# Four of eight condition sums as one-column products of TensorE, ahead of a hybrid attention and expert block

## The chip, the core and the metric

The kernel runs on one core of a Trainium2 chip. The metric is the device time of one execution in microseconds. A core has TensorE (PE in the rows, its weight loads as PEld), VectorE (DVE), ScalarE (ACT), GpSimd (POOL) and SyncE (SP), which issues most transfers; 16 DMA engines move the data.

## The reference

One transformer block for 512 tokens of 1,024 numbers. A condition c is turned into six rows; the first two shift and scale the first norm:

```
cs = silu(c)
mod = cs @ mod_w + mod_b
sh1, sc1, g1, sh2, sc2, g2 = split(mod, 6)
h = rms_norm(x, norm1_g) * (1 + sc1) + sh1
x = x + g1 * hybrid_mixer(h, w_in, ...)       # three kinds of attention, gates, output projection
h = rms_norm(x, norm2_g) * (1 + sc2) + sh2
x = x + g2 * moe_ffn(h, ...)                  # 32 experts, 4 for each token
return rms_norm(x, final_g)
```

mod_w is 1,024 x 6,144 in fp32. The case is about the first 2,048 of its columns: 1,024 sums for sh1 and 1,024 for sc1, each over 1,024 rows.

## The kernel before

**The condition.** `Mixer.start` (L743) loads the first 2,048 columns of mod_w in eight chunks of 1 MB: for each quarter k2 of the 1,024 columns first 256 scale columns, then 256 shift columns. So chunks 0, 2, 4 and 6 are scale, 1, 3, 5 and 7 are shift. The rows stand as eight pieces of 128 (k) on the partitions. Chunks 0, 1, 2, 4 and 6 lie in four small tiles each (z in the rows), 3 and 7 in p, 5 in o. For each chunk VectorE multiplies piece 0 by its column of cs (L786) and adds the other seven, each times its column, in seven scalar_tensor_tensor instructions (L784). This leaves a sum for each of 128 partitions; TensorE sums over the partitions by two fp32 products with a column of ones (L789), into columns of one tile `pc` in bank o. VectorE adds the bias (mc, L791) and, for scale columns, makes G1 = (1 + scale) * norm1_g (L793).

**What uses it.** x, normed by rows, is transposed by TensorE for each k (L798); ScalarE makes hT, the high part of (x * G1 + mc), for each k (L801), another instruction makes the full value (tp) and a subtraction the low part (L807). A quarter k2 gives two of the eight k.

**The projection.** Products of fp32 accuracy are made of three products of rounded fp32 parts (`mm3`, L632): high by high, low by high, high by low. `zT` (L944) makes one block of 128 columns: 8 k of 3 products, each 512 columns wide. The run (L1472) begins with four query blocks, two in banks z and two in banks s, then a key and a value block. Each needs its piece of w_in (raw), cast by ScalarE or VectorE to a high part and subtracted for a low one (`parts`, L814).

**Other work of VectorE.** `mod_steps` (L899) makes the other four rows of the condition in the same way, at a lower rank: eight steps of 1,024 columns for each row, from pieces called mraw, summed in acc.

**What sets the order.** All instructions up to the experts are first listed, then ordered by a planner (`Program.order`, L297). It simulates the engines with a list of prices (`price`, L263) and takes on each engine the earliest instruction that could start, by rank and then by place in the list; tiles get their place in the order in which they are first used (`access`, L243). The price of a product of plain fp32 is:

```
return max(0.107, n * 0.00168)
```

in us, for n columns. Every emitted instruction has line L417 in the profile. Banks: z has 2 places, s 3, t 2 (transposes), o 1. The bias columns of the projection are turned by TensorE in a bank s (L720).

After the mixer come the router and 32 experts, whose weights are streamed.

## Time and profile before

| | |
|---|---|
| median of 3 runs | 1854.42 us (1853.64 to 1858.9) |
| profiled execution | 1853.27 us, span 1851.3 us |
| PE busy | 1691.4 us (91%) |
| DVE busy | 1170.1 us (63%) |
| ACT busy | 764.9 us |
| POOL busy | 514.2 us |
| DMA | 512.38 MB, mean 277 GB/s |

Busy time is that of instructions on the engine; the ends of matmuls are modelled, and consecutive records overlap. [...]

### The profile page before, as it was taken

The page shows a single profiled execution, that of the slowest core. Times are in us where ns is not written, and L with a number is a line of the kernel's source. Part 1 is how long each engine was busy: PE and PEld are TensorE (multiplying, and loading weights), DVE is VectorE, ACT ScalarE, POOL GpSimd, SP SyncE. Part 2 cuts the span into 40 slices and gives each one's busy share as a digit, 9 for nine tenths or more (in the row PEclk, how much of TensorE's full clock was granted, in tenths as well). Part 3 has the DMA queues.
Part 4 walks back from the last instruction along what each step waited for, and adds up shares of the span by engine and source line. Part 5 has one row for each costly group of instructions (what it writes and reads, how often), then busy time and mean ns, then how long its engine had stood idle before and what let it go on. Part 6 is the DMA issues. An engine that isn't in the chain of part 4 may idle for free.

```text
span 1851.3 us, 22565 instructions
## 1 busy us (share of the span) xinstructions
PE 1691.4 (91%) x7923; PEld 1076.2 (58%) x7923; DVE 1170.1 (63%) x1797; ACT 764.9 (41%) x1081; POOL 514.2 (28%) x494
## 2 busy tenths in 40 slices
PE   4997999999999879897999998999899999989975
PEld 3776777777777766344445445455455455445654
DVE  7888768686865765346547546456475356435784
ACT  5473314474831234225426334335354235222652
POOL 5344202121212441311542221131131121412162
PEclk9999999999999979998999999999999999999997
DMA  9413465111133657999999999999999999999991
GB/s 323 153 61 114 117 198 164 58 46 58 47 95 103 238 191 283 402 398 377 374 397 399 340 363 352 385 376 395 404 387 354 363 372 394 373 402 407 408 358 47
DMA packets 156437, 512.38 MB, mean 277 GB/s; under 512 B 14266, under 2 KB 63545, under 8 KB 125601
## 3 DMA queue, kind: packets, MB, share of 16 engines
q1 hardware_dynamic: 146544, 486.65, 69.4%
q0 software_dynamic: 9136, 24.18, 5.4%
q8 instruction: 64, 1.05, 0.2%
q14 instruction: 53, 0.43, 0.1%
q10 hardware_dynamic: 640, 0.08, 0.0%
HBM read 492.81 MB, written 18.06 MB: 276 GB/s over the span
## 4 chain that ended last, share of the span: by engine, by line
PE 66%; DMA 14%; DVE 12%; ACT 4%; issue 2%; POOL 1%; SPq 0%; ACTq 0%; DVEq 0%; POOLq 0%
PE z L417 15%; PE hb L2041 7%; PE hb L1912 7%; PE hb L1914 6%; PE hb L1913 6%; DMA o<-in_exp_w_dram 6%; PE py L2041 5%; PE py L1914 3%; DMA raw<-in_exp_w_dram 3%; PE py L1912 3%; PE py L1913 3%; PE s L417 3%; DMA w<-in_exp_w_dram 2%; DVE z L417 2%; DVE p L417 2%
## 5 line engine op out<-in xcount | busy, mean ns | idle before, releaser
L417 PE MATMUL z<-hT,w 128*128 128x512 f32 (+1 forms) x1224 | 320.7, 403 | 3.3 <-DVE w L417 1.6
L417 PEld LDWEIGHTS z<-hT,w 128*128 128x128 f32 (+1 forms) x1224 | 225.2, 189 | 57.4 <-DVE w L417 3.5
L417 POOL TENSOR_TENSOR w<-raw,w 128x1024 fp32r<-128x1024 f32 (+2 forms) x32 | 63.6, 1990 | 160.6 <-ACT w L417 121.6
L1962 ACT CAST TH<-pt 128x512 fp32r<-128x512 f32 (+3 forms) x60 | 27.6, 510 | 189.4 <-PE pt L1961 189.4
L2041 PE MATMUL hb<-raw,T 128*64 128x512 f32 x448 | 102.8, 598 | 0.3 <-DMA raw<-in_exp_w_dram 0.3
L1912 PE MATMUL hb<-wh,TH 128*128 128x512 f32 (+3 forms) x256 | 103.1, 403 | 0.0
L1951 POOL DMA_INDIRECT xg<-dh,idp x33 | 39.6, 1199 | 221.7 <-PE hb L2041 114.9
L417 ACT ACTIVATE p<-p,sm 128x256 f32<-128x256 f32 (+3 forms) x171 | 89.1, 531 | 28.8 <-DVE sm L417 27.8
L1914 PE MATMUL hb<-wl,TH 128*128 128x512 f32 (+3 forms) x256 | 100.9, 394 | 0.0
L2158 POOL TENSOR_TENSOR mraw<-mraw,g 80x1024 f32<-80x1024 f32 (+3 forms) x12 | 33.3, 2778 | 243.0 <-ACT mraw L2157 243.0
L1913 PE MATMUL hb<-wh,TL 128*128 128x512 f32 (+3 forms) x256 | 100.7, 394 | 0.0
L1963 DVE TENSOR_TENSOR TL<-pt,TH 128x512 fp32r<-128x512 f32 (+3 forms) x60 | 32.8, 587 | 105.2 <-ACT TH L1962 105.2
L1856 DVE TENSOR_TENSOR wl<-raw,wh 128x2048 fp32r<-128x2048 f32 x38 | 90.1, 2374 | 13.8 <-ACT wh L1855 13.8
L1856 DVE TENSOR_TENSOR wl<-w,wh 128x2048 fp32r<-128x2048 f32 x28 | 64.0, 2288 | 33.1 <-ACT wh L1855 33.1
L1856 DVE TENSOR_TENSOR wl<-o,wh 128x2048 fp32r<-128x2048 f32 x29 | 67.3, 2321 | 22.0 <-ACT wh L1855 21.9
L2109 ACT ACTIVATE s<-g 128x512 f32<-128x512 f32 (+5 forms) x38 | 29.8, 788 | 124.3 <-DVE g L2105 124.3
L2193 POOL DMA_INDIRECT dacc<-mraw,sidx x16 | 41.4, 2585 | 138.3 <-DVE mraw L2068 138.3
L1855 ACT CAST wh<-raw 128x2048 fp32r<-128x2048 f32 x39 | 73.9, 1904 | 13.3 <-DMA raw<-in_exp_w_dram 12.6
L417 PE MATMUL z<-o,w 128*128 128x512 f32 x288 | 76.4, 399 | 0.3 <-DVE z L417 0.2
L417 ACT CAST w<-raw 128x512 fp32r<-128x512 f32 (+2 forms) x52 | 41.8, 808 | 80.2 <-PE z L417 67.2
L2112 POOL TENSOR_TENSOR g<-g,s 80x1024 f32<-80x1024 f32 (+5 forms) x21 | 42.9, 2047 | 113.4 <-ACT s L2109 113.3
L1856 DVE TENSOR_TENSOR p<-o,p 128x2048 fp32r<-128x2048 f32 x15 | 36.4, 2429 | 55.9 <-ACT p L1855 55.9
(532 smaller groups left out, 4079.9 us busy)
## 6 DMA issues: line engine op xcount, KB each, us to landing
raw<-in_exp_w_dram SPq DMA_DIRECT2D x154, 1024.0 KB, 13.2
o<-in_exp_w_dram SPq DMA_DIRECT2D x107, 1024.0 KB, 11.4
w<-in_exp_w_dram SPq DMA_DIRECT2D x107, 1024.0 KB, 13.1
raw<-in_w_in_dram SPq DMA_DIRECT2D x22, 1024.0 KB, 6.6
mraw<-in_mod_w_dram SPq DMA_DIRECT2D x32, 512.0 KB, 3.7
raw<-in_exp_w_dram SPq DMA_DIRECT2D x20, 512.0 KB, 9.4
z<-in_mod_w_dram SPq DMA_DIRECT2D x20, 256.0 KB, 7.0
mg<-in_x_dram SPq DMA_DIRECT2D x8, 512.0 KB, 3.3
```

The lines of the kernel that those rows point to most:

```text
L417: f(*[real(x) for x in op.a], **{n: real(x) for n, x in op.k.items()})
L1855: nc.scalar.copy(H, raw)
L1856: getattr(nc, eng).tensor_sub(L, raw, f32(H))
L1912: mm(out, aH, bH, start=start, stop=False)
L1913: mm(out, aL, bH, start=False, stop=False)
L1914: mm(out, aH, bL, start=False, stop=stop)
L1951: self.nc.gpsimd.indirect_dma_start(out=x, out_offset=None, in_=self.dram["h2"], in_offset=bass.IndirectOffsetOnAxis(ap=idx[:n], axis=0))
L1963: nc.vector.tensor_sub(L, pt, f32(H))
L2041: self.nc.tensor.matmul(out[n * 64:n * 64 + 64], x, w[:, n * 512:n * 512 + 512], start=start, stop=stop)
L2112: getattr(nc, mul).tensor_mul(g, g, s)
L2158: nc.gpsimd.tensor_mul(y, y, g2)
L2193: self.nc.gpsimd.indirect_dma_start(out=acc, out_offset=bass.IndirectOffsetOnAxis(ap=idx, axis=0), in_=y, in_offset=None, compute_op=ALU.add)
```

## The change

The scale chunks stay as they are. For a shift chunk VectorE's eight instructions go; TensorE multiplies the raw pieces itself. For each half m of the 256 columns it makes eight fp32 products, piece k (128 x 128) as weights and column k of cs as the one moving column, summed in a bank s; VectorE adds the bias from there.

```
@@ -779,16 +779,22 @@
             for s in (1, 0):
                 raw = raws.pop(0)
                 acc = raw[0]
-                for k in range(KT):
+
+                o = s * 8 + k2 * 2
+                ps = pc[:, o:o + 2] if s else self.bank("s", [2])
+                for k in range(KT if s else 0):
                     if k:
                         nc.vector.scalar_tensor_tensor(acc, raw[k], self.cs[:, k:k + 1], acc, op0=ALU.mult, op1=ALU.add)
                     else:
                         nc.vector.tensor_scalar(acc, acc, self.cs[:, 0:1], None, op0=ALU.mult)
                 for m in range(2):
-                    o = s * 8 + k2 * 2 + m
-                    nc.tensor.matmul(pc[:, o:o + 1], acc[:, m * 128:m * 128 + 128], self.ones[:, 0:1], start=True, stop=True)
-                o = s * 8 + k2 * 2
-                nc.vector.tensor_add(mc[:, o:o + 2], pc[:, o:o + 2], self.cols[:, R_MB + o:R_MB + o + 2])
+                    ms = slice(m * 128, m * 128 + 128)
+                    if s:
+                        nc.tensor.matmul(ps[:, m:m + 1], acc[:, ms], self.ones[:, 0:1], start=True, stop=True)
+                        continue
+                    for k in range(KT):
+                        nc.tensor.matmul(ps[:, m:m + 1], raw[k][:, ms], self.cs[:, k:k + 1], start=k == 0, stop=k == KT - 1)
+                nc.vector.tensor_add(mc[:, o:o + 2], ps, self.cols[:, R_MB + o:R_MB + o + 2])
```

## Rows read from the trace of the kernel before

**Rows 1.** Windows (us from the start): busy time of each engine, granted clock, DMA.

```profile
10.00:31.00 21.00, 8.27 (x33) 6.22 (x33) 17.62 (x41) 9.93 (x15) 11.68 (x30) 1.00 1.09 344
31.00:38.00 7.00, 4.76 (x15) 3.13 (x14) 6.92 (x12) 4.53 (x8) 4.90 (x12) 1.00 1.11 349
38.00:54.00 16.00, 15.04 (x72) 11.68 (x72) 15.84 (x40) 5.37 (x10) 9.47 (x67) 0.87 0.73 242
54.00:62.00 8.00, 8.00 (x25) 6.44 (x26) 4.73 (x12) 2.37 (x4) 1.55 (x3) 0.62 0.56 197
62.00:80.00 18.00, 18.00 (x79) 14.41 (x77) 16.53 (x19) 7.84 (x11) 6.63 (x6) 1.00 0.32 95
80.00:640.00 560.00, 532.09 (x2629) 413.43 (x2628) 425.68 (x968) 251.87 (x628) 145.74 (x118) 0.99 0.36 110
```

**Rows 2.** Timeline of VectorE: start, length, instruction, idle before it.

```profile
23.73 0.35 DVE L417 TENSOR_SCALAR p<-p,cs 128x256 f32<-128x256 f32 x1 [0.79 <-DMA p<-in_mod_w_dram]
...
31.08 0.16 DVE L417 TENSOR_TENSOR mc<-o,cols 128x2 f32<-128x2 f32 x1
...
51.36 0.47 DVE L417 SCALAR_TENSOR_TENSOR z<-z,cs,z 128x256 f32<-128x256 f32 x1
51.76 0.47 DVE L417 SCALAR_TENSOR_TENSOR p<-p,cs 128x256 f32<-128x256 f32 x1
...
55.39 0.15 DVE L417 SCALAR_TENSOR_TENSOR G<-mc,cols 128x2 f32<-128x2 f32 x1
```

**Rows 3.** Timeline of TensorE.

```profile
30.03 1.01 PE L417 MATMUL o<-ones,p 128*128 128x1 f32 x4 [4.27 <-DVE p L417]
30.91 0.77 PE L417 MATMUL z<-hT,w 128*128 128x512 f32 x1
...
38.20 0.61 PE L417 MATMUL o<-ones,z 128*128 128x1 f32 x4 [1.82 <-DVE z L417]
...
45.21 1.09 PE L417 MATMUL s<-hT,o 128*128 128x512 f32 x4
...
79.84 0.22 PE L417 MATMUL s<-z,z 128*128 128x128 f32 x1
```

**Rows 4.** Groups of TensorE from 59 to 80.

```profile
L417 PE MATMUL z<-hT,w 128*128 128x512 f32 x60 | 15.0, 405 | 0.0
L417 PE MATMUL s<-hT,o 128*128 128x512 f32 x29 | 7.5, 404 | 0.0
```

**Rows 5.** Waits of TensorE from 28 to 80: total, times, longest.

```profile
PE o L417 <- DVE p L417: 4.3, 1, 4.3
PE o L417 <- DVE z L417: 2.6, 2, 1.8
```

**Rows 6.** Group of VectorE from 11 to 55: busy, mean ns.

```profile
L417 DVE SCALAR_TENSOR_TENSOR p<-p,cs 128x256 f32<-128x256 f32 x14 | 8.6, 614 | 0.1
```

**Rows 7.** Timeline of SP: issues of transfers.

```profile
35.81 0.89 SPq L417 DMA_DIRECT2D z<-in_mod_w_dram  x2
```

**Rows 8.** Window from 46 to 47, columns as in rows 1.

```profile
46.00:47.00 1.00, 1.00 (x9) 0.83 (x7) 1.00 (x2) 1.00 (x2) 1.00 (x1) 1.00 0.10 35
```

**Rows 9.** Timeline of TensorE behind the mixer: runs of small products.

```profile
672.82 1.42 PE L417 MATMUL s<-tp,z 128*128 128x32 f32 x12
...
685.49 1.91 PE L2305 MATMUL pn<-sel,ones 128*128 128x32 f32 x8
```

**Rows 10.** Instructions on acc from 50 to 130: ns min/median/max, first, last start.

```profile
L417 DVE SCALAR_TENSOR_TENSOR acc<-mraw,cs,acc x7: 1270/1277/2397, 55.5 to 92.4; 128x1024 f32<-128x1024 f32 x7
```

**Rows 11.** Waits of TensorE from 80 to 350.

```profile
PE t L417 <- DVE p L417: 5.4, 5, 1.5
```

**Rows 12.** Window from 678 to 680, columns as in rows 1.

```profile
678.00:680.00 2.00, 0.01 (x1) 0.01 (x1) 2.00 (x9) 0.30 (x2) 2.00 (x4) 0.50 0.99 394
```

**Rows 13.** Timeline of ScalarE.

```profile
28.03 1.12 ACT L417 CAST w<-raw 128x512 fp32r<-128x512 f32 x2
...
44.31 0.78 ACT L417 ACTIVATE hT<-t,mc,G 128x512 fp32r<-128x512 f32 x1 [3.79 <-DVE mc L417]
```

## The prediction

> **What bounds the stage now.** I read the windows of the first 80 us first. [rows 1] VectorE (DVE) is busy 6.92 of the 7 us from 31 to 38 and 15.84 of the next 16; TensorE (PE) only 8.27 of the 21 us up to 31 and 4.76 of the 7 behind. So the condition looks like a VectorE stage, and until 38 it is one. But from 38 to 54 TensorE is busy 15.04 of 16, and from 54 to 80 it has no gap at all.

> Then VectorE's timeline. [rows 2] The steps of the condition follow each other every 0.40 us (51.36, 51.76), a record lasting 0.47; the last G1 is made at 55.39.

> Then TensorE's. [rows 3] The first large product of the projection starts at 30.91, right behind two column sums, and the first score comes at 79.84. The four query blocks, the key and the value block hold 6 x 24 = 144 products of 512 columns. Of these 60 + 29 = 89 still run behind 59 [rows 4], by when G1 has been ready for 3.5 us; only 6 of each block's 24, or 36, need the last two k of hT. TensorE's large waits from 28 to 80 are 4.3 us, which end at 30.03, and 2.6 in two, of which 1.8 end at 38.20 [rows 3, 5]; none of them is for hT. This is the point on which the forecast turns: VectorE's end at 55 is not what TensorE waits for. TensorE is late by its own work.

> **The change part by part.**

> Removed from VectorE: four chunks of one tensor_scalar (0.35 us) and seven steps (0.40): 4 x (0.35 + 2.8) = 12.6 us, 9.5 of it in the three chunks from 23.73 on [rows 2]. Some steps are longer: the p form means 614 ns over 14 [rows 6] against 0.47. I let that excess pass to VectorE's next instruction; should it vanish instead, VectorE wins 14 x 0.14 = 2 us more.

> How much earlier can the last G1 be? SP issues the last two scale pieces at 35.81 [rows 7], and traffic, at 349 GB/s up to 38, is down to 35 at 46 [rows 1, 8]: they have landed by then. Four steps (1.6 us), two sums (0.6) and two small additions (0.3) put G1 at about 48, so hT's last two k some 7.5 us earlier. TensorE has the older products to do there, and I price the gain at nothing; if that cover were gone (TensorE idle at 48), it would be worth up to those 7.5 us.

> Added on TensorE: 4 x 16 = 64 fp32 products of one column, for 8 removed. Four records, two weight loads and two matmuls for each of two sums, take 1.01 us at 30.03 and 0.61 at 38.20 [rows 3]: 0.25 us a matmul record early on, 0.153 later. This includes the tail of the last one; twelve 32-column products in a row take 1.42 us (0.118 each), and eight at the low clock 1.91 (0.24) [rows 9]. A product is two records. [...]

> [...]

> Chunks 1 and 3 (the first and second pair of k) come while TensorE idles 21 - 8.27 = 12.7 us [rows 1]. Their 64 - 8 = 56 extra records cost 56 x 0.23 = 12.9 there. That just fits, but not where it matters: chunk 3 lands at 23.73 (VectorE waited for it) [rows 2]; its 32 records take 4.2 us (fast) to 8 (slow), and some 2.4 of transposes and scale sums stand between: 30.3 to 34. Its shift columns were added at 31.08 before, and the first large product started at 30.91 [rows 2, 3]. I take a start 1 us later (ends: 0.6 earlier, 3 later).

> Chunks 5 and 7 come behind 31, where TensorE is nearly full: again 56 extra records, 56 x 0.13 = 7.3 us (6.6 to 8.6 at the high clock, 11 to 14 at the low).

> Given back: TensorE's idle time behind 31, 7 - 4.76 = 2.2 and 16 - 15.04 = 1.0, together 3.2 [rows 1]. The 2.2 lie mostly ahead of the third scale sum at 38.20, which waited for VectorE 1.8 [rows 3], and I let all of it go (ends: 1 to 3.2).

> VectorE's freed time later: the seven 1.28 us steps of the second condition, 9.0 us, run from 55.5 to 93 [rows 10] and could begin near 46. Behind 80 TensorE waits for VectorE's p 5.4 us in 270 [rows 11]. I take 1.5 back (0 to 4).

> Sum at TensorE: 1.0 + 7.3 - 3.2 - 1.5 = +3.6 us. The granted clock I leave as it was: 0.87 over 16 us and 0.62 over 8 [rows 1] lose 16 x 0.13 + 8 x 0.38 = 5.1 us.

> Other edits. The shift columns leave bank o for bank s, whose three places had three users (the bias transposes, two query blocks) and now have seven in line; the last waits until chunk 7's columns are read, near 47, where the first s products came at 45.21 [rows 3]. One block 2 us late while z blocks are there: nothing, at most 2. The pieces of chunk 1 are held until the second m has read them, some 5 us longer, but the two transfers that need a freed place were issued only at 35.81 [rows 7]: nothing, at most their 0.9. And the planner, which writes the order of all that comes before the experts, lists an fp32 product of one column at 0.107 us where I read 0.24 to 0.5. It will place them too early, and every new order shifts small waits; TensorE idles 28 us between 80 and 640 [rows 1], so I allow 4 us either way.

> The profiled run took 1853.27 us for a span of 1851.3, and lies 1.15 under the median of 1854.42. So 1856.9 by the run, 1858.0 by the median; I say 1857.

> **Rivals.**

> A, the forecast: the work goes to where TensorE is full. +3.6, own range 0 to +7. Chance 0.46.

> B, the clock falls. TensorE ran small products almost without a gap from 672.8, then idled, and stood at half clock (0.50) from 678 to 680 [rows 9, 12]. One-column products of chunks 5 and 7, sixteen in a row, could bring the same: each chunk then costs 32 x (0.23 - 0.13) = 3.2 us, and 3 us of large products behind it at half speed another 1.5. That is +8.3 with one fall, +13 with both. It decides once a fall comes on top of those in the profile; against it, these may only move. Chance 0.16; 1862 to 1867.

> C, the stage was VectorE's after all. ScalarE had cast the first w by 29.15, and hT's third pair of k waited 3.8 us until 44.31 for VectorE's columns [rows 13]; with both earlier the large products begin earlier and closer together, the 7.5 us pass to the end, and 1847 comes out. It decides if TensorE has nothing left at 48. Against it: the 89 products due behind 59. Chance 0.18.

> D, the products hold the clock up. TensorE would be at work almost throughout from 16 on, and the 5.1 us lost to the clock and 2 more of slow records near 31 come back: 3.6 - 7 = -3.4, 1851. [...] Chance 0.20.

> **How the numbers follow.** 0.3% is 5.6 us, about what a measurement of this kernel can tell from no change. Slower by more: B whole and 0.14 of A, its upper end with a worse order: 0.30. Faster by more: C nearly whole (0.15) and 0.06 of D: 0.21. Within: the rest, 0.49. The likeliest is A, 1857, own range 1854 to 1861. For 8 in 10 the range reaches to C's 1847 and to the middle of B, 1865.

> **What would show it.** Right: 128 one-column records from raw pieces and 16 from scale sums, 32 VectorE instructions gone, the last G1 near 48, and yet the first score near 83, with hardly a gap of TensorE behind 40. Wrong: the first score before 78 (C if the gaps ahead of 48 are what went, D if the low clock went), or granted clock 0.5 right behind the products of chunks 5 and 7 and the first score behind 87 (B). If the first score comes as forecast and the total differs by more than 5 us, the order further on did it.

## The result, and the profile after

The changed kernel takes 1870.87 us (median of six runs, 1865.9 to 1873.96), the kernel before beside it 1854.03 (1847.99 to 1858.9): a ratio of 1.0089, interval 1.0067 to 1.0111, so 12.4 to 20.6 us slower. The forecast of 1857 and its upper end of 1865 are both passed.

Two marks are used below: the first score, which is the start of the first product s<-z,z of the attention, and the routing product behind the mixer (hb, L2024).

The windows of the changed kernel, with the stretches and columns of [rows 1]:

```profile
10.00:31.00 21.00, 18.46 (x83) 16.86 (x83) 9.78 (x23) 8.74 (x13) 11.13 (x26) 1.00 1.10 347
31.00:38.00 7.00, 6.35 (x26) 4.81 (x26) 5.83 (x11) 5.37 (x9) 4.05 (x6) 1.00 1.11 349
38.00:54.00 16.00, 14.47 (x68) 13.69 (x68) 12.03 (x26) 3.30 (x5) 8.71 (x75) 0.59 0.54 176
54.00:62.00 8.00, 8.00 (x34) 7.10 (x35) 5.40 (x18) 2.39 (x5) 3.34 (x8) 0.54 1.00 363
62.00:80.00 18.00, 18.00 (x79) 14.50 (x78) 14.70 (x15) 5.13 (x7) 0.00 (x0) 1.00 0.44 125
```

VectorE is relieved indeed: 9.78 busy of 21, then 5.83 of 7 and 12.03 of 16, where it had 17.62, 6.92 and 15.84. But the granted clock, a share of full speed, has gone from 0.87 to 0.59 between 38 and 54, and from 0.62 to 0.54 between 54 and 62. The timeline of TensorE, for [rows 3], says where:

```profile
25.27 6.83 PE L417 MATMUL s<-cs,p 128*128 128x1 f32 x32
...
33.03 0.77 PE L417 MATMUL z<-hT,w 128*128 128x512 f32 x1 [0.63 <-DVE w L417]
...
37.23 1.26 PE L417 MATMUL s<-cs,o 128*128 128x1 f32 x10
40.02 0.61 PE L417 MATMUL o<-ones,z 128*128 128x1 f32 x4 [1.53 <-DVE z L417]
40.49 4.53 PE L417 MATMUL s<-cs,o 128*128 128x1 f32 x22
...
48.44 6.82 PE L417 MATMUL s<-cs,p 128*128 128x1 f32 x32
...
58.18 10.28 PE L417 MATMUL z<-hT,w 128*128 128x512 f32 x37
68.30 11.38 PE L417 MATMUL s<-hT,o 128*128 128x512 f32 x48
79.51 11.36 PE L417 MATMUL z<-hT,w 128*128 128x512 f32 x48
90.71 1.23 PE L417 MATMUL s<-z,z 128*128 128x128 f32 x10
```

The first ten records of chunk 5 cost 0.126 us each, the next 22 cost 0.206 and chunk 7's 32 cost 0.213. Of the 144 large products of the projection only 11 stand ahead of 58, and 37 + 48 + 48 = 133 behind; the first score comes at 90.71, 10.9 later than in [rows 3]. The window over the slow part, and the waits of VectorE from 10 to 60:

```profile
40.00:61.00 21.00, 20.98 (x93) 19.57 (x94) 15.47 (x39) 5.70 (x10) 10.16 (x74) 0.52 0.66 224
```

```profile
DVE mc L417 <- PE s L417: 12.7, 4, 5.4
DVE mc L417 <- PE o L417: 4.4, 4, 2.0
```

For 21 us TensorE is busy without a pause at a mean granted clock of 0.52. And VectorE, in its fixed order, now stands 12.7 us behind TensorE's shift sums: each addition of two columns to mc waits in its queue until the chunk's 32 records are through. Its timeline shows the longest of these waits, and the last G1:

```profile
32.13 0.16 DVE L417 TENSOR_TENSOR mc<-s,cols 128x2 f32<-128x2 f32 x1 [5.40 <-PE s L417]
...
57.60 0.15 DVE L417 SCALAR_TENSOR_TENSOR G<-mc,cols 128x2 f32<-128x2 f32 x1
```

The last G1 is at 57.60, not near 48 and not even at the 55.39 of before [rows 2].

**The balance from 31 to the first score.** TensorE's idle time falls from 3.2 to 0.65 + 1.53 = 2.2: -1.0. The clock loses 20.98 x 0.48 = 10.1 us where it lost 5.1: +5.0. The start of the large products is 2.1 us later (33.03 against 30.91), but of that only chunk 3's last records behind 31 are added work, some 1 us (five at 0.213); a pause of 0.63 is in the idle time already. Together 5.0 of 10.9, and 5.9 are left for the 56 added records. At 0.12 each, their price at the full clock (late, below), they would be 6.7; 0.8 us of gain is not assigned. So the loss is about half the clock's and half the work's.

### The profile page after: what moved, and what is told of

It reads as the page before. It is cut to its first block, busy times and chain, and to the rows that moved or that the text cites. A ratio compares the mean times of both kernels' runs of the same rounds, so it can differ in the third digit from the quotient of the medians.

```text
span 1869.2 us, 22747 instructions
## 1 busy us (share of the span) xinstructions
PE 1719.8 (92%) x8035; PEld 1107.4 (59%) x8035; DVE 1166.5 (62%) x1777; ACT 760.4 (41%) x1074; POOL 508.4 (27%) x489
## 4 chain that ended last, share of the span: by engine, by line
PE 69%; DMA 12%; DVE 11%; ACT 4%; issue 2%; POOL 1%; SPq 0%; ACTq 0%; DVEq 0%; POOLq 0%
PE z L417 17%; PE hb L2047 7%; PE hb L1918 6%; PE hb L1920 6%; PE hb L1919 6%; DMA o<-in_exp_w_dram 5%; PE py L2047 5%; PE s L417 4%; DMA raw<-in_exp_w_dram 3%; PE py L1920 3%; PE py L1918 3%; PE py L1919 3%; DMA w<-in_exp_w_dram 2%; PE t L417 2%; PE o L417 2%
## 6 DMA issues: line engine op xcount, KB each, us to landing
o<-in_exp_w_dram SPq DMA_DIRECT2D x107, 1024.0 KB, 12.7
```

## The experiments

Where a total is told, the kernel before ran beside it.

**The change repeated** (no edit).

> The changed kernel itself, a second profile. The first one lost 10.9 us by the first score (90.71 against 79.84) and some 9 more behind 350, where the granted clock was 0.50 in stretches near 358 to 370, 411 to 415 and 497 to 507 that have no counterpart in the kernel before. If the order of the instructions makes these falls, they stand at the same places again; if they hang on chance, some are gone or others have come, and only the first loss, the first score at 90.7 within 0.5, is the same.

1875.73 us, first score 91.27 (0.56 from 90.71), half clock from 41 to 61 again. The changed kernel's first score is 91.0 on the mean. The falls behind 350 come back within 4 us too (granted clock 0.52 from 362 to 365.5, 0.50 from 413.5 to 420 and from 502.2 to 508.8), so they go with the order of the instructions at least in part.

**Relief alone.** Its shift columns are sums over two of the eight pieces. The routing then follows other values and the expert part does other work, so its total (1919.74) says nothing, and only the time up to the first score is read.

```
-                    for k in range(KT):
+                    for k in (0, 7):
```

> Leaves work out: of the eight products of each half of a shift chunk only those of pieces 0 and 7 are made, so TensorE makes 16 one-column products in place of 64, while VectorE has all the relief of the change. Theory 1 (TensorE's products are the cost, VectorE's end was not the bound): first score between 76 and 81, time within 4 us of the kernel before. Theory 2 (the new waits in VectorE's queue and the new order are the cost, whatever the products take): first score 86 or later, time still 10 us or more above. Rival C of the prediction (VectorE was the bound): first score near 72, time 7 us below.

First score 73.70, 6.1 us earlier than before and between the first theory's 76 and rival C's 72; last G1 49.9. TensorE from 31 to the first score, in before and then in relief, and two rows of relief's timeline:

```profile
31.00:79.84 48.84, 45.64 (x186) 35.66 (x186) 43.89 (x81) 20.09 (x30) 22.55 (x86) 0.90 0.61 196
```

```profile
31.00:73.70 42.70, 41.99 (x185) 34.31 (x184) 35.13 (x64) 15.74 (x25) 16.60 (x79) 1.00 0.70 225
```

```profile
36.44 2.48 PE L417 MATMUL z<-hT,w 128*128 128x512 f32 x5
...
40.70 2.44 PE L417 MATMUL z<-hT,w 128*128 128x512 f32 x9
```

TensorE's idle time there is 42.70 - 41.99 = 0.7 us where it was 3.2: 2.5 of the 6.1. Another part is the clock's: it doesn't fall from 41 to the first score, where the kernel before lost 5.1 us to two falls; against that, relief's first slow stretch is longer (at 36.44 a large product still takes 0.5 us, from 40.70 on 0.27, and the 1.00 of the row says nothing of it). How much of the clock's part is VectorE's doing was not tried.

**Chunks 1 and 3 alone**, then **chunks 5 and 7 alone**, as products; the others stay VectorE's.

```
+ early: ps = pc[:, o:o + 2] if s or k2 > 1 else self.bank("s", [2])
+ late:  ps = pc[:, o:o + 2] if s or k2 < 2 else self.bank("s", [2])
         (the loops over k and m with the same condition)
```

> Only chunks 1 and 3 go to TensorE, 5 and 7 stay with VectorE. If the cost lies in the products that come behind 31 us, where TensorE has projection products to make (theory 1), the first score comes at 79 to 83 and the time is within 4 us of the kernel before. If the early products already push everything back, by the chain from chunk 3 to hT and the first weights, the first score is at 85 or later.

> Only chunks 5 and 7 go to TensorE, 1 and 3 stay with VectorE: the other half of the kernel early, whose first score came at 79.48. If the cost is the products behind 31 us, at the low clock and ahead of the projection in TensorE's queue, this half carries it: first score 86 to 92, granted clock 0.5 in most of 38 to 60, time 8 us or more above the kernel before. If it takes both halves together, the first score is below 84.

Early: 1859.82, ratio 1.0018 (0.9994 to 1.0042), first score 79.48. Late: 1862.92, ratio 1.0054 (1.0029 to 1.0079), first score 87.97. Of the loss of 91.0 - 79.2 = 11.8 us up to the first score (79.2 is the mean of the 79.84 of before and the 78.56 of its second profile, below) the two chunks where TensorE is full bring 8.8 by themselves, the other two 0.3. The timeline of the late kernel, and its windows:

```profile
38.20 4.41 PE L417 MATMUL s<-cs,o 128*128 128x1 f32 x20
...
46.01 3.85 PE L417 MATMUL s<-cs,p 128*128 128x1 f32 x32
...
53.81 8.43 PE L417 MATMUL z<-hT,w 128*128 128x512 f32 x24
```

```profile
38.00:49.00 11.00, 11.00 (x61) 10.36 (x61) 7.81 (x17) 3.30 (x5) 3.65 (x17) 1.00 0.74 254
49.00:59.00 10.00, 8.92 (x35) 7.42 (x35) 7.57 (x23) 2.39 (x5) 6.30 (x45) 0.51 0.90 303
```

Chunk 5's records still ran at half speed (0.22 each at 38.20, though the row has 1.00). Chunk 7 ran at 0.12 a record, the price at the full clock; the clock fell as it ended, and the large products paid: 24 in 8.43 us, 0.35 each at a granted clock of 0.51, where 0.237 is the rate at 1.00 (48 in 11.36 above).

**Is it the order?** The planner lists the product at its price of the low clock (price); the products stand at a lower rank (lowrank).

```
+ price:   if self.dear: return 0.43      (set around the loop over k)
+ lowrank: nc.rank = 1 ... nc.rank = 0    (around the same loop)
```

> The whole change, but the planner lists each of the 64 products at 0.43 us, near what the profile shows (32 records in 6.83 us), in place of 0.107. If the order written with the wrong price is the cost, TensorE and VectorE get an order without the long waits and the first score comes at 80 to 84, the time within 6 us of the kernel before. If the work itself is the cost, the first score stays at 88 to 91 and the time 11 us or more above.

> The whole change, but the shift products have a lower rank in the planner's choice, so that of TensorE's work that can start the projection goes first: in the order as written the 32 records of chunks 5 and 7 stand behind some 20 products of the projection in place of 5. If their place in the queue is the cost, the clock stays up and the first score comes at 80 to 84. If the work alone is the cost, at 88 or later.

Price: 1887.51, ratio 1.0187 (1.0145 to 1.0228), first score 107.19. Lowrank: 1878.24, ratio 1.0126 (1.0088 to 1.0164), first score 95.80. My theory that a mispriced product is placed too early fell: both are worse. The order written for price puts every large product behind the last chunk:

```profile
70.97 13.97 PE L421 MATMUL z<-hT,w 128*128 128x512 f32 x48
```

Up to there TensorE ran only short records, the condition's and transposes, with pauses of 5 to 7 us for VectorE, all of them at half speed though the row has 1.00: from 31 to 39, 47 to 55 and 62 to 69 six or seven records lie in each us, as in after from 49 to 54, where one takes 0.213 us; in late from 46 to 49, at 0.12 a record, there are eleven. In lowrank chunk 5 ran 32 records in 3.63 us from 48.17, and the clock fell behind it all the same (0.51 from 52 to 62); chunk 7 ran from 69.94, and it fell again (0.50 from 72.7 to 79.5). So no order tried was better. An order could at most give back the clock's part and the 2.2 us of idle time that are left.

**Products added, nothing removed** (the kernel before, with the 64 products beside VectorE's steps; nobody reads their sums).

```
+                if not s:
+                    ps = self.bank("s", [2])
...
+                            nc.tensor.matmul(ps[:, m:m + 1], keep[k][:, ms], self.cs[:, k:k + 1], start=k == 0, stop=k == KT - 1)
```

> The kernel before, with VectorE's 64 steps all kept, and the 64 one-column products made beside them into a bank that nobody reads (the product of piece 0 uses piece 1): the work on TensorE without the relief of VectorE. The kernel relief had the reverse, with a first score at 73.70, 6.1 earlier than before. If the two effects add, the products alone bring 10.9 + 6.1 = 17 us and the first score comes at 95 to 99. If the relief is worth nothing once the products are there, it comes at 90 to 92, as in the changed kernel.

1873.89, ratio 1.0108 (1.0072 to 1.0144), first score 93.86, half clock from 40 to 64. Neither theory's range holds it: it lies between adding up (95) and no gain (92). The change without its relief costs 2.9 us more at the first score than with it, and a part of that is the eight records of VectorE's sums that this kernel keeps behind 31; so at most 3 of the relief's 6 us survive beside the products.

**The products by themselves**: the kernel before, with one chunk's 16 products (sum unread) inside its densest stretch, where the clock of before is 1.00 from 62 to 80 [rows 1].

```
         run(self.zk(R_KV, ka))
+        ps = self.bank("s", [2])
+        for m in range(2):
+            for k in range(KT):
+                self.nc.tensor.matmul(ps[:, m:m + 1], f32(self.hTH[:, 7, m * 128:m * 128 + 128]), self.cs[:, k:k + 1], ...)
```

> The kernel before, with 16 one-column products of fp32 added in the midst of dense work: behind the first key block, weights from hT, where the granted clock was 1.00 from 60 on. If 0.21 us a record is the price whatever the clock, the 32 records take 6.8 us; if it is the clock's, 3.8 to 4.9 us. If a run of such products makes the clock fall, the granted clock is 0.5 within some us behind them; in the kernel before it stayed at 1.00 from 60 to 145.

Timeline of TensorE, then windows:

```profile
70.31 4.14 PE L417 MATMUL s<-cs,hT 128*128 128x1 f32 x32
74.31 8.44 PE L417 MATMUL z<-hT,w 128*128 128x512 f32 x24
82.58 1.23 PE L417 MATMUL s<-z,z 128*128 128x128 f32 x10
```

```profile
70.00:73.00 3.00, 3.00 (x28) 2.91 (x27) 2.65 (x5) 1.22 (x2) 1.27 (x1) 1.00 0.59 187
73.00:80.00 7.00, 7.00 (x23) 5.74 (x22) 6.05 (x5) 1.74 (x3) 1.08 (x1) 0.52 0.41 115
```

This is the cleanest view of the fall. TensorE is busy 3.00 of 3 and 7.00 of 7 us; nothing waits; and from 73 on, while the last of the 32 one-column records run, the granted clock stands at 0.52. The chunk costs 4.1 us itself, and 24 large products behind it 8.44 instead of 24 x 0.237 = 5.7: 2.7 more. The first score, at 82.58, is for all that only 2.7 later than 79.84, mostly since the fall that the kernel before shows between 54 and 62 (0.62) is not in this profile (1.00). It is one execution, of 1858.1 us; but the clock fell in or behind a run of some 30 such records each time that records just ahead of the fall were short (0.11 to 0.13 us each): in after, in late, in lowrank twice, and here.

**The same sums in another form.** The condition's column is loaded and 256 columns of the raw piece pass; ScalarE copies the row out, and one-element products turn it into columns.

```
+                    row = self.bank("s", [512])
+                    for k in range(KT):
+                        nc.tensor.matmul(row[0:1, 0:256], self.cs[:, k:k + 1], raw[k], start=k == 0, stop=k == KT - 1)
...
+                    nc.scalar.copy(rs1, row[0:1, 0:256])
```

> The changed kernel with the two operands exchanged: the condition's column is what is loaded and 256 columns of the raw piece pass, so a shift chunk is 8 products of 256 columns into a row, which ScalarE copies out and two one-element products turn into columns. Theory 'clock' (long runs of one-column products let the granted clock fall): with wide products in their place the clock does not fall behind chunks 5 and 7, a chunk costs 2 to 4 us instead of 6.8, and the first score comes at 80 to 86 instead of 90.71. Theory 'work and waits' (TensorE is late by the time and the waits that the chunks bring, in whatever form): first score 88 to 94, granted clock 0.5 to 0.6 from 40 to 60 as in the changed kernel.

1852.52, ratio 0.9992 (0.9972 to 1.0013), first score 78.52. Timeline and windows:

```profile
23.14 3.61 PE L417 MATMUL s<-p,cs 128*1 128x256 f32 x16
...
36.74 3.18 PE L417 MATMUL s<-o,cs 128*1 128x256 f32 x14
...
44.44 3.61 PE L417 MATMUL s<-p,cs 128*1 128x256 f32 x16
```

```profile
38.00:54.00 16.00, 16.00 (x87) 10.57 (x86) 13.72 (x33) 7.39 (x13) 6.92 (x64) 1.00 0.88 294
54.00:62.00 8.00, 8.00 (x36) 6.45 (x35) 6.94 (x12) 3.76 (x6) 5.46 (x8) 1.00 0.10 36
```

A chunk takes 16 records and 3.61 us, hardly less than the 3.85 of 32 one-column records at the full clock. The granted clock is 1.00 from 38 to 62, and the whole loss is gone. The work is not: 32 records behind 31 at 0.226 are 7.2 us. But the two falls of the kernel before (5.1 us) are not there, only a shorter one (0.76 from 31 to 38), and TensorE idles 0.9 us from 31 to the first score in place of 3.2. The same sums on the same engine cost 17 us or nothing, by their form. (The order that the planner makes differs too; the next pair keeps two chunks as before.)

**The row form in chunks 5 and 7 alone** (against late), **and in chunks 1 and 3 alone.**

```
+ rowlast:  if not s and k2 > 1:   row = ...
+ rowearly: if not s and k2 < 2:   row = ...
```

> The row form in chunks 5 and 7 alone, the counterpart of the run with one-column products there (first score 87.97, ratio 1.0054, granted clock fallen behind chunk 7). Theory 'clock': no half-clock stretch behind either chunk, first score 79 to 82, ratio 0.998 to 1.002. Theory 'work and waits': first score 85 to 88, ratio 1.004 to 1.006 as with one-column products.

> The row form in chunks 1 and 3 alone; chunks 5 and 7 are VectorE's as before. VectorE loses 6.3 us of steps, TensorE gets 32 records of 256 columns into its idle time ahead of 31 us and nothing behind. Theory 'TensorE's own work from 38 on sets the first score': 75 to 78.5, total 1847 to 1852. Theory 'VectorE's waits on the columns eat it': first score 79 to 81, total 1853 to 1856, same.

Rowlast: 1858.88, ratio 1.0013 (0.9992 to 1.0034), first score 83.45. That is between the two theories, 1.45 above the range of the first. Late lost 4.5 us more up to there, and its 8.92 busy us at 0.51 lose 8.92 x 0.49 = 4.4 (the slow records of chunk 5, 0.22 each in late from 38.20 and 0.44 in rowlast from 38.17, differ a little too, so the match is partly luck). Here are rowlast's windows over the stretch where late's clock fell:

```profile
38.00:49.00 11.00, 11.00 (x40) 4.42 (x40) 8.19 (x19) 5.17 (x10) 3.50 (x26) 1.00 0.92 311
49.00:59.00 10.00, 10.00 (x59) 8.19 (x58) 8.34 (x21) 3.82 (x7) 6.25 (x33) 1.00 0.69 243
```

The rest of late's delay, 83.45 - 79.2 = 4.2 us, is what the form does not change: 32 added records (7.2 us at 0.226 each), less what idle time and clock give back. Rowearly: 1854.38, ratio 0.9992 (0.9973 to 1.001), first score 77.30; its two earlier microseconds don't show in the total.

**Chunk 1 alone as one-column products** (the condition k2 > 0 in place of early's).

> The changed kernel with the products in chunk 1 alone; chunks 3, 5 and 7 are VectorE's as before. Theory 'clock': these 32 records lie in TensorE's idle time ahead of 31 us and touch no dense stretch, VectorE is relieved of 3.15 us from 17 us on; first score 76.5 to 79 (before 79.84), total 1850 to 1856, same or a little faster. Theory 'adding and queue': VectorE's wait for the products eats the relief, first score 79.5 to 81, total 1854 to 1858.

1852.91, ratio 0.9994 (0.9977 to 1.0011), first score 80.43: no gain, no loss, as by the second theory; VectorE waits 2.9 us for the 32 records.

**The part behind the first score.** TensorE's order is the same in both kernels from some 53 us behind the first score to the routing product, yet the part from the first score on took 604.5 us before (79.84 to 684.34) and 615.6 after (90.71 to 706.28). So the kernel before was profiled again, and once with 48 dense products of 512 columns (sum unread) behind the first key block.

```
+        ps = self.bank("s", [512])
+        for j in range(48):
+            self.nc.tensor.matmul(ps, self.hTH[:, 7, 0:128], self.hTH[:, j % KT], start=j == 0, stop=j == 47)
```

> The kernel before, unchanged, a second time. Open is why the stretch from the first score to the routing product, where TensorE's order is the same in both kernels, took 604.5 us in the one profile of the kernel before and 612 to 622 in every other profile so far. Theory 'one draw': where TensorE's clock falls in that stretch differs from execution to execution, and the profile of before had few falls; then this one takes 608 to 616 us from score to route, with half-clock stretches near 344, 400 or 489 us. Theory 'the shift': a later start moves the falls, and the kernel before repeats itself; then 603 to 606 us, first score 79.6 to 80.2, route 683.5 to 686.

> The kernel before with 48 dense products of 512 columns, whose sum nobody reads, behind the first key block: about 11 us of TensorE at the full clock, no one-column product added and no step of VectorE changed. Theory 'the shift': what comes behind is the later by more than these 11 us, score to route 612 or more as in the changed kernel, though nothing of the change is in it. Theory 'the products': without one-column products the stretch keeps its 604.5 us, and route comes near 684.3 + 11 = 695.5. First score 88 to 92 by both.

> The kernel before with 48 dense products behind the first key block again, timed. One look gave a first score 9.3 us later and a total 13 us over the median of before. Theory 'the later start costs more further on': the ratio shows 12 to 16 us (1.0065 to 1.0086), above the delay itself. Theory 'it is the draw of one execution': the ratio shows the delay alone, 8 to 11 us (1.0043 to 1.0060), and the rest of the changed kernel's 16.8 us, some 5 us, then belongs to the change.

The kernel before, again: first score 78.56, total 1858.01, and the routing product here:

```profile
694.75 1.23 PE L2024 MATMUL hb<-mraw,selc 64*128 64x512 f32 x4 [0.34 <-DVE idx L417]
```

That is 616.2 us for the same stretch of the same kernel. Its windows, where the first profile of before shows 1.00 in all three:

```profile
395.00:402.00 7.00, 7.00 (x28) 5.93 (x27) 5.65 (x27) 4.51 (x17) 0.00 (x0) 0.56 0.50 153
484.00:491.00 7.00, 7.00 (x28) 5.95 (x27) 5.77 (x27) 4.51 (x17) 0.00 (x0) 0.54 0.48 150
658.00:668.00 10.00, 10.00 (x40) 8.74 (x39) 4.99 (x17) 2.84 (x7) 3.46 (x4) 0.54 0.67 211
```

For this part the profile of before was a favourable draw. Of the 17 profiles of this case 15 take 612.1 to 622.5 us for it; only before (604.5) and the row form (604.7) take less. Two of these falls stand at nearly the same place in all 15, 315 to 325 and 404 to 413 us behind the first score, with the change or without; the row form has only the second, before neither. So such a fall belongs to the place in the program, and an execution can miss it. Behind the routing product the profile of before was in turn slow (1167.0 us to the end, 1161.3 in its second profile), and its total, 1853.27, is near the median.

One dense delay, in a single execution: first score 89.11, routing 704.24, total 1866.93. Timed: 1864.49, ratio 1.0043 (1.0024 to 1.0063), that is 4.4 to 11.7 us for a delay of 89.43 - 79.2 = 10.2. A later start costs itself and, within the interval, at most 1.5 us more.

## Why the prediction was wrong

**The step that failed** is "The granted clock I leave as it was", and with it the price of chunks 5 and 7 in "56 x 0.13 = 7.3 us". The clock's loss, held at 5.1 us, was 10.1. The price of a record was right where the clock was up (0.12 in late, 0.13 in the lone chunk, 0.126 in the first ten records after), but the clock fell with the products (0.52 in after from 40 to 61, in lone from 73 to 80), and then they ran at 0.21 themselves. That was rival B, to which I gave 0.16; its sign, granted clock near 0.5 behind the two chunks and a first score behind 87, is what the profile shows. The lone chunk shows the fall without any wait, and the row form that it comes with the form and not with the sums. Even B's 1862 to 1867 was low: I counted 3 us of large products behind each chunk at half speed, and the stretch at half clock lasted from 40 to 61. The 0.13 and 0.23 us a record in these sums were my choice, and no run shows 0.23: the runs show 0.12 to 0.13 at a granted clock of 1.00, and 0.21 to 0.22 at 0.50 and in the early records.

A second term was mis-sized: of the idle time "given back", 3.2 us of which I took all, only 1.0 came. By the sum's own terms the first score would have been 79.84 + 1.0 + 7.3 - 3.2 = 84.9; "near 83" takes in the 1.5 us that the sum gets back only behind 80. From 84.9, the clock's 5.0 and the 2.2 of idle time not given back make 92.1; the first profile has 90.71.

**What I read the wrong way round** was the evidence. I had the row of small products from 672.8 with half clock at 678 [rows 9, 12], and set against it that the falls "may only move". In after they lengthened, from 10 us of half clock ahead of the first score to some 20; in lone they moved.

**VectorE's gain.** "I price the gain at nothing" is not refuted as clearly as the 6.1 us of relief suggest: 2.5 of them are idle time of TensorE, which the forecast has under "given back", and much of the rest is the clock's. Beside the real products at most 3 are left (both against after). So rival C's mechanism is there, but smaller than the products' cost. TensorE was late by its own work, by the clock, and by the few us that the condition kept from it.

**G1.** "Near 48" failed, at 57.60: I counted VectorE's removed steps and not its new waits. An addition of two columns that reads TensorE's sum stands in VectorE's queue until the sum is there, 12.7 us in all, and the steps of the next scale sums stand behind it. In the row form it is 50.92.

**Right or nearly so.** Chunks 1 and 3 cost little: a start 2.1 us later where I took 1 (ends -0.6 and 3), and nothing at the first score when alone (early). The idle time given back was 1.0, the lower end of 1 to 3.2. The two other orders tried were worse, so a wrong price in the planner is not the cause; that the order has no share is not shown. Rival D is refuted for this form: one-column products did not hold the clock up (0.52 in after from 40 to 61). In the row form the account came out as in D: a work of 7.2 us, near the 7.3 of the forecast, was paid by the clock (1.00 from 38 to 62, where before has 0.87 and 0.62) and the idle time (0.9 us in place of 3.2). That its products held the clock up is not shown.

A product is two records, 32 for the 16 of a chunk. Late's chunk 7 took 3.85 / 16 = 0.24 us a product at a granted clock of 1.00, after's 6.82 / 16 = 0.43 at 0.50. In the row form a record of 256 fp32 columns takes 0.226 us, nearly as long as one of 512 columns in the rounded parts (0.237), both at 1.00; why was not tried.

**What stays open.** The total is 16.8 us slower and the first score 91.0 - 79.2 = 11.8 later. 11.8 lies just below the interval's lower end of 12.4. shift5 doesn't give the 5 us between to the delay; both of after's profiles have a part behind the first score (615.6 and 619.4) like that of the second profile of before (616.2), and against that profile after's span is 13.2 us longer (1869.2 against 1856.0), 12.15 of them there at the first score. I can't say whether the 5 us belong to the change; the 1.5 us that the forecast got back behind 80 are not seen. Why the clock falls with one-column records (1.00, then 0.52 in lone) was not tried beyond their form. The row form changes the order of the instructions too; no run has it in the order of the one-column products.

## What to carry to other kernels

Here the price of moving work to TensorE lay nearly as much in what the granted clock did (5.0 of the 10.9 us at the first score) as in the work itself (5.9): ask whether the new instructions are of the kind that the engine ran at full clock before, and cost those behind them at either level. A sum over partitions with one column can be turned round so that many columns pass; here, with 256, that took away the whole loss (ratio 0.9992 in place of 1.0089). And when an engine hands a sum to another, add the consumer's wait in its own fixed queue, here 12.7 us of VectorE, to the account before counting its freed steps.
